# Delta-rule state without its zero blocks: 64-row products, accumulators banked by head, one state update

## Chip, core and metric

The kernel runs on one core of a Trainium2 chip. The metric is the device time of one execution in microseconds (us): 1829.12 us, the median of three runs (1828.71 to 1832.35).

## What is computed

The reference is a two-layer decoder trunk on 1024 tokens of width 1024, in float32: an RWKV-7 time-mixing layer, then a differential-attention layer, each followed by a gated per-layer input embedding (a matrix product, a sigmoid, a product), and a last RMSNorm. The change touches the recurrence of the first layer alone. There, 16 heads of 64 carry a 64 by 64 state from token to token:

```python
def step(state, inp):
    r_t, w_t, k_t, v_t, kk_t, b_t = inp
    sa = jnp.einsum('bhij,bhj->bhi', state, kk_t)
    state = (state * w_t[:, :, None, :] - sa[..., None] * b_t[:, :, None, :]
             + v_t[..., None] * k_t[:, :, None, :])
    y_t = jnp.einsum('bhij,bhj->bhi', state, r_t)
    return state, y_t
...
_, y = lax.scan(step, s0, ...)
mean = jnp.mean(y, axis=-1, keepdims=True)
var = jnp.mean(jnp.square(y - mean), axis=-1, keepdims=True)
y = ((y - mean) * lax.rsqrt(var + GN_EPS) * ln_w.reshape(H, N) + ln_b.reshape(H, N))
...
return (y * jax.nn.silu(gate)) @ w_out
```

## The kernel before

The recurrence is done in 16 chunks of 64 tokens. Inside a chunk the steps become matrix products (the delta rule's chunked form); between chunks the state is carried. The 16 heads stand as two sets (`st` 0 and 1) of four pairs (`p_`) of two heads (`h`). A pair's two states lie as two diagonal 64 by 64 blocks of one 128 by 128 block of the tile `state[st]`, and the two blocks beside them are zero.

One chunk `c` has three steps in a fixed order:

- `chain_x(c)`: the state's products (L855) write a chunk's accumulators `xy` (one 2 KB bank of PSUM for each set), and products of the chunk's masked key matrix `m` with the values `vu` are added (L864). POOL forms `spl`, the decayed state (L875), and ACT copies the result `x` out (L878).
- `chain_u(c)`: `x` is multiplied by the inverse `ti` (L890), and DVE scales the result into `vu` (L895).
- `chain_s(c)`: the new state's products `s` (L906), the state update on DVE (L910, four instructions of 64 partitions), the output's products into the other halves of `xy` (L916), and the copies of the output `y` (L923, ACT).

Other work is woven between these steps by lists with costs, and a scheduler then sets each engine's order. Two kinds matter here. `stage1(st, c + 1)` prepares the next chunk: transposes `kbt` of the keys (L175, copied by ACT into `kbn`, L176), the products `pm` (L185), which DVE masks into `m` (L188), and transposes `prt` of a key product (L162), which DVE sums into `bon` (L166). `d1_pieces` takes the outputs of two chunks, 128 tokens, after each odd chunk: a group norm on DVE (`norm`: L953 to L955, then ACT squares `y` into `ysq`, L957; `norm2`: a sum L963, twelve small instructions on 128 by 16 for the reciprocal root, L68 and L58 to L65, the scaling L966), POOL multiplies by `lnw` (L967), DVE adds (L970). Two chunks later `turn` transposes this (`ytr`, L981), DVE forms `sg` (L984), ACT and DVE split it into `gh` and `gl` (L71, L72), and 48 matmuls `op` (L75 to L77) multiply by `w_out`. Their sum is added to `x` (`xr`, L997), and ACT squares it (`h1sq`, L1001). The first chunks have 96 matmuls `pps` of another product in the place of `op`.

The tiles `pm`, `kbt`, `prt` and `ytr` share two PSUM banks (tag `t`, `bufs=2`), so each waits until the one two places ahead of it is read. Every engine runs its instructions in its program's order:

```python
pm = [ps1[0].tile([P, 4, P], F32, tag=ps1[1], name=f"pm{h}{u}", bufs=2) for h in range(2)]
...
ps = pp.tile([P, 4, P], F32, tag="t", name=f"ytr{i}{hf}", bufs=2)
```

Of the kernel before, what the change touches and what calls it, by code (L numbers as in the profile page):

```python
# [11 lines left out]
F32 = mybir.dt.float32  # L12
# [25 lines left out]
def trunk(ctx: ExitStack, tc: tile.TileContext, A, out):  # L38
# [725 lines left out]
                                       op0=ALU.mult, op1=ALU.subtract)  # L764

    def proj_N(pp, nm, ah, al, w, tag="mm", bufs=4, by_row=False, parts=2, tick=lambda n: None):
        pss = [pp.tile([P, 512], F32, tag=tag, name=f"{nm}{hf}", bufs=bufs) for hf in range(2)]
# [48 lines left out]
    with NB("d") as d, NP("psco") as pp:  # L816
# [25 lines left out]

        def chain_x(c):

            px_, ms = [], []
            vu2 = vus.pop(c)
            if c + 1 < NCH:
                vload(c + 1)
            for st in range(2):
                kkr, kbn, m = units[st, c]  # L850
                vu = vu2[:, st]
                px_.append(pp.tile([P, 4, 2, L], F32, tag="xy", name=f"xy{st}_{c}", bufs=2))
                ctx_c[st] = (half_(st), half_(1 - st), vu, px_[st])
                with tc.high_priority():
                    ms += [T.matmul(px_[st][:, p_].rearrange("p h l -> p (h l)"), lhsT=kkr[:, p_],  # L855
                                    rhs=state[st][:, p_], start=(p_ == 0), stop=False, skip_group_check=True)
                           for p_ in range(4)]
            with tc.high_priority():
                for p_ in range(4):
                    for h in range(2):  # L860
                        for st in (1, 0):
                            xs_, ys_, vu, px = ctx_c[st]
                            m = units[st, c][2]
                            ms.append(T.matmul(px[xs_, p_, h], lhsT=m[ys_, h, p_, half_(st)], rhs=vu[ys_, p_, h],  # L864
                                               start=False, stop=True, skip_group_check=True))
            turns(ms)
            x = co.tile([P, 4, 2, L], F32, tag="x", name=f"x{c}", bufs=1)
            for st in range(2):
                xs_, ys_, vu, px = ctx_c[st]
                spl = None  # L870
                if c < NCH - 1:
                    spl = co.tile([P, 4, L], F32, tag="spl", name=f"spl{st}_{c}", bufs=2)
                    for h in range(2):
                        hs = half_(h)
                        G.tensor_tensor(out=spl[hs], in0=state[st][hs, :, hs],  # L875
                                        in1=plast[hs, 4 * st:4 * st + 4, c:c + 1].to_broadcast([64, 4, L]),
                                        op=ALU.mult)
                S.copy(x[xs_], px[xs_])  # L878
                ctx_c[st] += (spl, x)

        def chain_u(c):
            ti = tis[c // 4]
            pu = [pp.tile([P, 4, 2, L], F32, tag="us", name=f"u{st}_{c}", bufs=2) for st in range(2)]
            ms = []
            with tc.high_priority():
                for p_ in range(4):
                    for h in range(2):
                        for st in (1, 0):
                            xs_, x = ctx_c[st][0], ctx_c[st][5]
                            ms.append(T.matmul(pu[st][xs_, p_, h], lhsT=ti[xs_, (c % 4) * 8 + h * 4 + p_],  # L890
                                               rhs=x[xs_, p_, h], start=True, stop=True))
            turns(ms)
            for st in range(2):
                xs_, vu = ctx_c[st][0], ctx_c[st][2]
                V.tensor_tensor(out=vu[xs_], in0=pu[st][xs_],  # L895
                                in1=rn[xs_, c].rearrange("p h j -> p j h").unsqueeze(3).to_broadcast([64, 4, 2, L]),
                                op=ALU.mult)

        def chain_s(c):
            ms = []  # L900
            if c < NCH - 1:
                for st in range(2):
                    vu, spl, kbn = ctx_c[st][2], ctx_c[st][4], units[st, c][1]
                    pS = pp.tile([P, 4, L], F32, tag="us", name=f"s{st}_{c}", bufs=2)
                    with tc.high_priority():
                        ms += [T.matmul(pS[half_(h), p_], lhsT=kbn[:, p_, half_(h)], rhs=vu[:, p_, h],  # L906
                                        start=True, stop=True) for p_ in range(4) for h in range(2)]
                    for h in range(2):
                        hs = half_(h)
                        V.tensor_tensor(out=state[st][hs, :, hs], in0=pS[hs], in1=spl[hs], op=ALU.add)  # L910
            with tc.high_priority():
                for p_ in range(4):
                    for h in range(2):
                        for st in (1, 0):
                            xs_, ys_, vu, px = ctx_c[st][:4]
                            ms.append(T.matmul(px[ys_, p_, h], lhsT=units[st, c][2][:, h, p_, half_(1 - st)],  # L916
                                               rhs=vu[:, p_, h], start=False, stop=True, skip_group_check=True))
            turns(ms)
            po = (c % 2) * 64
            for st in range(2):  # L920
                ys_, px = ctx_c[st][1], ctx_c[st][3]
                units.pop((st, c))
                S.copy(D1[c // 2]["y"][po:po + 64, st * 512:st * 512 + 512], px[ys_].rearrange("p j h l -> p (j h l)"))  # L923

        D1, wo = {}, {}

# [708 lines left out]
```

## Time and profile before

| | |
|---|---|
| median of three runs | 1829.12 us |
| the profiled execution | 1828.3 us, span 1826.5 us |
| busy: PE (matmul) | 1684.7 us, 92% of the span |
| busy: DVE | 1350.9 us, 74% |
| busy: ACT | 760.4 us, 42% |
| busy: POOL | 634.5 us, 35% |
| mean granted TensorE clock | 0.963 of full speed |
| first and last L906 (new state's products) | 602.29 and 886.37 us |

The profile is one execution. An instruction's row gives its start, its duration, its engine and line, the tile it writes and those it reads; where its engine stood idle ahead of it, the row names what ended that. A float32 matmul of the program is two passes in the trace, so 16 matmuls show as x32. Matmuls overlap each other, so their spacing is read from the rows' spans and not from one duration.

### The profile page before, as it was taken

How to read it: one execution, taken by the hardware profiler on the slowest of the kernel's cores; microseconds unless marked ns; L12 is line 12 of the kernel's file. 1: busy time of each engine (PE TensorE's matmuls, PEld its weight loads, DVE VectorE, ACT ScalarE, POOL GpSimd, SP SyncE). 2: the span in 40 equal slices, each digit the busy share in tenths (PEclk: the TensorE clock that was granted, in tenths of full speed). 3: DMA queues.
4: the chain of work that ended last, by engine and by line, in shares of the span. 5: the costliest groups of instructions: out<-in, count | busy, mean ns of one | idle time of the engine just before them, and what ended most of it. 6: DMA issues, size and time to landing. Idle time of an engine off the chain costs nothing.

```text
span 1826.5 us, 30473 instructions
## 1 busy us (share of the span) xinstructions
PE 1684.7 (92%) x11320; PEld 1397.6 (77%) x11320; DVE 1350.9 (74%) x3083; ACT 760.4 (42%) x1594; POOL 634.5 (35%) x705
## 2 busy tenths in 40 slices
PE   6899999898897988898899999899999999999998
PEld 5677778887676877777678878788888888777786
DVE  7878954698994687666766747887877878856665
ACT  6566543346344332223333434444444444544332
POOL 4436644224324355455310333323323323311200
PEclk9999999998998989999999999999999999999999
DMA  7125444434225534444243411101101101431121
GB/s 267 41 61 166 129 106 109 125 102 119 73 67 186 186 127 127 122 129 131 97 172 128 132 51 39 54 7 56 56 7 56 53 10 56 154 99 34 58 93 69
DMA packets 164401, 175.97 MB, mean 96 GB/s; under 512 B 74845, under 2 KB 127837, under 8 KB 164254
## 3 DMA queue, kind: packets, MB, share of 16 engines
q1 hardware_dynamic: 161950, 169.84, 30.2%
q10 hardware_dynamic: 2304, 4.20, 0.6%
q8 instruction: 89, 1.46, 0.4%
q14 instruction: 58, 0.48, 0.1%
HBM read 124.19 MB, written 49.81 MB: 95 GB/s over the span
## 4 chain that ended last, share of the span: by engine, by line
PE 51%; DVE 10%; ACT 2%; issue 1%; DMA 0%; POOL 0%; ACTq 0%; DVEq 0%
PE qkv L75 6%; PE qkv L76 6%; PE qkv L77 6%; PE av L1359 3%; PE sc L1319 2%; PE sc L1320 2%; PE fg L75 2%; PE fg L76 2%; PE fg L77 2%; PE op L75 2%; PE op L77 2%; PE op L76 2%; PE do L75 1%; PE pg L76 1%; PE pg L77 1%; PE do L76 1%
## 5 line engine op out<-in xcount | busy, mean ns | idle before, releaser
L1329 ACT ACTIVATE e<-sc,mx 128x256 f32<-128x256 f32 (+7 forms) x128 | 94.0, 738 | 111.0 <-DVE mx L1326 60.0
L1273 POOL TENSOR_TENSOR rp<-rp,rq 128x128 f32<-128x128 f32 x64 | 34.8, 543 | 237.6 <-DVE rq L1268 189.7
L1359 PE MATMUL av<-vh,aT 128*128 128x128 f32 x576 | 81.1, 280 | 6.3 <-DVE aT L1355 6.3
L1359 PEld LDWEIGHTS av<-vh,aT 128*128 128x128 f32 x576 | 75.6, 195 | 12.8 <-DVE aT L1355 8.9
L1325 DVE TENSOR_REDUCE mxs<-sc 128x1 f32<-128x128 f32 (+6 forms) x112 | 74.2, 682 | 0.5
L1319 PE MATMUL sc<-k,q 128*128 128x512 f32 (+2 forms) x192 | 71.5, 379 | 2.2 <-ACT e L1329 2.2
L229 DVE SCALAR_TENSOR_TENSOR xmt<-hT,cB,xmt 128x512 f32<-128x512 f32 x64 | 63.5, 1012 | 6.6 <-ACT xmt L228 6.3
L1320 PE MATMUL sc<-k,q 128*128 128x512 f32 (+2 forms) x192 | 64.8, 348 | 0.0
L1361 ACT ACTIVATE o<-av,r 128x128 f32<-128x128 f32 x64 | 23.5, 367 | 88.4 <-PE av L1359 88.4
L875 POOL TENSOR_TENSOR spl<-state,plast 64x256 f32<-64x256 f32 x60 | 41.4, 690 | 49.6 <-DVE state L910 42.7
L1341 DVE SCALAR_TENSOR_TENSOR e<-e,r,e 128x128 f32<-128x128 f32 (+3 forms) x64 | 56.5, 883 | 1.2
L560 DVE TENSOR_TENSOR tb<-tb,tm 128x31 f32<-128x31 f32 (+15 forms) x124 | 53.9, 435 | 3.6
L558 DVE TENSOR_TENSOR tm<-tb,nb 128x31 f32<-128x31 f32 (+15 forms) x124 | 53.9, 434 | 3.6
L188 DVE TENSOR_TENSOR m<-pm,mmask 128x512 f32<-128x512 f32 x64 | 41.1, 682 | 20.0 <-PE pm L185 19.7
L1301 POOL CAST q<-q 64x128 fp32r<-64x128 f32 x128 | 38.5, 302 | 49.4 <-PE sc L1320 45.6
L1267 DVE TENSOR_TENSOR rp<-qkv,rc 128x256 f32<-128x256 f32 x64 | 27.1, 423 | 38.3 <-PE qkv L77 30.1
L1292 POOL CAST k<-k 64x256 fp32r<-64x256 f32 x64 | 26.1, 408 | 83.7 <-ACT k L1290 82.5
L185 PE MATMUL pm<-kkr,kb 64*128 64x128 f32 x512 | 50.8, 307 | 3.1 <-ACT kbn L176 2.2
L1355 DVE COPY aT<-at 128x512 f32<-128x512 f32 (+2 forms) x96 | 52.0, 550 | 1.1 <-PE at L1353 0.4
L185 PEld LDWEIGHTS pm<-kkr,kb 64*128 64x128 f32 x512 | 40.4, 203 | 12.9 <-issue 6.0
L1353 PE MATMUL at<-ident,e 128*128 128x128 f32 x288 | 47.4, 277 | 2.8 <-DVE e L1341 2.3
L923 ACT COPY y<-xy 64x512 f32<-64x512 f32 x32 | 18.6, 580 | 71.4 <-PE xy L916 71.0
(1180 smaller groups left out, 6001.5 us busy)
## 6 DMA issues: line engine op xcount, KB each, us to landing
pp_d<-ppo SPq DMA_DIRECT2D x32, 256.0 KB, 2.3
kb_d<-kb SPq DMA_DIRECT2D x16, 512.0 KB, 2.6
kkr<-kkr_d SPq DMA_DIRECT2D x32, 256.0 KB, 3.2
kb<-kb_d SPq DMA_DIRECT2D x32, 256.0 KB, 3.3
x<-in_x SPq DMA_DIRECT2D x8, 512.0 KB, 5.5
kkr_d<-ep SPq DMA_DIRECT2D x16, 256.0 KB, 2.6
kkr_d<-rt SPq DMA_DIRECT2D x16, 256.0 KB, 2.6
bb<-kb_d SPq DMA_DIRECT2D x32, 128.0 KB, 2.6
```

Source lines behind the costliest of these rows:

```text
L75: T.matmul(ps, lhsT=ah, rhs=bh, start=start, stop=False)
L76: T.matmul(ps, lhsT=ah, rhs=bl, start=False, stop=False)
L77: T.matmul(ps, lhsT=al, rhs=bh, start=False, stop=stop)
L185: ms.append(T.matmul(pm[h][:, p_], lhsT=kb[hs, p_], rhs=kkr[hs, p_], start=True, stop=True))
L229: V.scalar_tensor_tensor(out=t, in0=hT[:, kt, half(hf)], scalar=cB[:, g, kt:kt + 1], in1=t, op0=ALU.mult, op1=ALU.add)
L558: V.tensor_tensor(out=tv, in0=tb[:, j:j + 1, 0:w].to_broadcast([P, n, w]), in1=nb[:, j + 1:32, j:j + 1].to_broadcast([P, n, w]), op=ALU.mult)
L1319: T.matmul(ps[:, b0:b1], lhsT=q1[:, m, ts_], rhs=k1[:, m, b0:b1], start=True, stop=False)
L1320: T.matmul(ps[:, b0:b1], lhsT=q0[i % 2][:, m], rhs=k2[:, b0:b1], start=False, stop=True)
L1325: V.tensor_reduce(out=seed, in_=ps[:, 0:n - P], axis=AX.X, op=ALU.min)
L1329: S.activation(e[:, 0:n], ps[:, 0:n], AF.Exp, scale=-1.0, bias=mx, accum_out=l_[:, m:m + 1])
L1341: V.scalar_tensor_tensor(out=es[0][:, 0:n], in0=es[1][:, 0:n], scalar=r[:, 1:2], in1=es[0][:, 0:n], op0=ALU.mult, op1=ALU.add)
L1359: T.matmul(po, lhsT=aT[kb // 4][:, kb % 4], rhs=c["vh"][:, kb], start=(kb == 0), stop=(kb == i))
```

## The change

The tile `state` holds only the diagonal blocks: 128 partitions (the two heads of a pair in the lower and the upper 64) by two sets, four pairs and 64 columns. The state's products become 16 matmuls on 64 rows and 64 columns in place of 8 on 128 and 128, the two heads in turns. The accumulators `xy` are one tile of two banks, split by head and no longer by set, with `bufs=1`. The state update, and `spl` on POOL, become one instruction on 128 partitions each. The copies of `x` and `y` read across the two banks. `proj_N` takes a two-bank tile where its tag is `xy`.

```diff
-        state = []
-        for st in range(2):
-            s_ = co.tile([P, 4, P], F32, name=f"state{st}")
-            G.memset(s_, 0.0)
-            state.append(s_)
+        state = co.tile([P, 2, 4, L], F32, name="state")
+        G.memset(state, 0.0)
...
-                px_.append(pp.tile([P, 4, 2, L], F32, tag="xy", name=f"xy{st}_{c}", bufs=2))
...
-                    ms += [T.matmul(px_[st][:, p_].rearrange("p h l -> p (h l)"), lhsT=kkr[:, p_],
-                                    rhs=state[st][:, p_], start=(p_ == 0), stop=False, skip_group_check=True)
-                           for p_ in range(4)]
+            px = pp.tile([P, 2, 2, 4, L], F32, tag="xy", name=f"xy{c}", bufs=1)
             with tc.high_priority():
...
+                for st in range(2):
+                    kkr = units[st, c][0]
+                    for p_ in range(4):
+                        for h in range(2):
+                            ms.append(T.matmul(px[:, h, st, p_], lhsT=kkr[half_(h), p_], rhs=state[half_(h), st, p_],
+                                               start=(st == 0 and p_ == 0), stop=False, skip_group_check=True))
+                for h in range(2):
+                    for p_ in range(4):
+                        for st, h_ in ((1, h), (0, 1 - h)):
+                            ms.append(T.matmul(px[half_(st), h_, st, p_],
+                                               lhsT=units[st, c][2][half_(1 - st), h_, p_, half_(st)],
+                                               rhs=vu2[half_(1 - st), st, p_, h_],
                                                start=False, stop=True, skip_group_check=True))
             turns(ms)
...
+                spl = co.tile([P, KT, L], F32, tag="spl", name=f"spl{c}", bufs=2)
+                G.tensor_tensor(out=spl, in0=state.rearrange("p s j l -> p (s j) l"),
+                                in1=plast[:, :, c:c + 1].to_broadcast([P, KT, L]), op=ALU.mult)
...
-                    for h in range(2):
-                        hs = half_(h)
-                        V.tensor_tensor(out=state[st][hs, :, hs], in0=pS[hs], in1=spl[hs], op=ALU.add)
+                pS = pp.tile([P, 2, 4, L], F32, tag="us", name=f"s{c}", bufs=2)
...
+                V.tensor_tensor(out=state, in0=pS, in1=spl.rearrange("p (s j) l -> p s j l", s=2), op=ALU.add)
```

The scheduler also orders the work around these steps anew. Three places in the recurrence show it; numbers in a tile's name tell its chunk and its buffer, and the changed kernel's line numbers differ by a few (L855 is now L856, L864 is L861, L890 is L886, L906 is L901, L916 is L908, L923 is L916, L966 is L959).

The first is DVE's queue in chunk 6, an even chunk, behind the sum `gst<-ysq` of the group norm. `gst` are the norm's small statistics, `m_6` the mask products that chunk 6's L864 reads. Before:

```order
L963 TENSOR_REDUCE gst_7046<-ysq_7050 128x16
L188 TENSOR_TENSOR m_6_6625<-pm_6_6755,mmask 128x512
L188 TENSOR_TENSOR m_6_6625<-pm_6_6754,mmask 128x512
L68 TENSOR_SCALAR gst_7046<-gst_7046 128x16
L984 SCALAR_TENSOR_TENSOR sg_6601<-ytr_6825,vecs,sg_6601 128x128 x4
L58 TENSOR_SCALAR gst_7046<-gst_7046 128x16
L60 TENSOR_SCALAR gst_7046<-gst_7046 128x16
```

Now, after the sum and nine of the twelve small instructions:

```order
L63 TENSOR_TENSOR gst_7037<-gst_7037 128x16
L64 SCALAR_TENSOR_TENSOR gst_7037<-gst_7037 128x16
L65 SCALAR_TENSOR_TENSOR gst_7037<-gst_7037 128x16
L959 TENSOR_TENSOR y_6408<-y_6408,gst_7037 128x1024
L188 TENSOR_TENSOR m_6_6618<-pm_6_6751,mmask 128x512
L188 TENSOR_TENSOR m_6_6618<-pm_6_6750,mmask 128x512
L963 TENSOR_TENSOR y_6408<-y_6408,vn_7031 128x1024
L977 SCALAR_TENSOR_TENSOR sg_6594<-ytr_6817,vecs,sg_6594 128x128 x4
```

The two `m` have moved from directly behind the sum to behind all twelve small instructions and the scaling of `y` (L966, now L959), and `sg` to behind the addition L970 (now L963). Chunks 2, 4, 12 and 14 now read the same; in chunks 8 and 10 seven small instructions stand ahead of the first `m`, one between the two, and the scaling behind them. Before, `m` stood directly behind the sum in chunks 6, 8, 12 and 14, ahead of the sum in 4 and 10, and behind one and two small instructions in 2.

The second is PE's queue at the entry of chunk 7, an odd chunk. Before, behind the last product of chunk 6 (here a matmul of L916):

```order
L916 MATMUL xy_6_6867<-vu_6627,m_6_6621 64x64
L162 MATMUL prt_7_6940<-ident,pr_7_6937 128x128 x2
L175 MATMUL kbt_7_6975<-ident,kbp_7_6973 128x128 x4
L76 MATMUL op_6912<-rwo7l,gh_6783 128x512
L77 MATMUL op_6912<-rwo7h,gl_6784 128x512
L77 MATMUL op_7116<-rwo0h,gl_6784 128x512
```

Then 16 more `op`, the state's products, and the eight `pm`, of which the last two open this piece:

```order
L185 MATMUL pm_7_7029<-kkr_7_6860,kb_7_6861 128x128
L185 MATMUL pm_7_7028<-kkr_7_6860,kb_7_6861 128x128
L76 MATMUL op_7116<-rwo6l,gh_6783 128x512
L77 MATMUL op_7116<-rwo6h,gl_6784 128x512
L75 MATMUL op_7116<-rwo7h,gh_6783 128x512
L76 MATMUL op_7116<-rwo7l,gh_6783 128x512
L77 MATMUL op_7116<-rwo7h,gl_6784 128x512
L162 MATMUL prt_7_7055<-ident,pr_7_7052 128x128 x2
L864 MATMUL xy_7_7076<-vu_6864,m_7_6862 64x64
```

Now:

```order
L76 MATMUL op_7110<-rwo7l,gh_6779 128x512
L77 MATMUL op_7110<-rwo7h,gl_6780 128x512
L856 MATMUL xy_7062<-state,kkr_7_6848 128x64 x8
L856 MATMUL xy_7062<-state,kkr_7_6852 128x64 x8
L162 MATMUL prt_7_6935<-ident,pr_7_6932 128x128 x2
L175 MATMUL kbt_7_6970<-ident,kbp_7_6968 128x128 x4
L185 MATMUL pm_7_7020<-kkr_7_6852,kb_7_6853 128x128
L185 MATMUL pm_7_7019<-kkr_7_6852,kb_7_6853 128x128
```

All 48 `op` now stand ahead of the state's products (19 of them already ahead of chunk 6's L890, 21 behind it, 8 behind L916). `prt` and `kbt` have moved behind the state's products, directly ahead of `pm`, and behind the eight `pm` come only `prt` and the L864 products (now L861).

The third is ACT's queue from the output copies of chunk 4 to the first `kbn` of chunk 6. Before:

```order
L923 COPY y_6414<-xy_4_6431 64x512
L923 COPY y_6414<-xy_4_6426 64x512
L176 COPY kbn_5_6422<-kbt_5_6534 128x512
L1001 ACTIVATE h1sq_6752,ss_5440<-xr_6127 128x1024
L878 COPY x_6656<-xy_5_6635 64x512
L878 COPY x_6656<-xy_5_6630 64x512
L176 COPY kbn_6_6622<-kbt_6_6669 128x512
```

Now:

```order
L916 COPY y_6408<-xy_6420 64x2x4x64 x2
L994 ACTIVATE h1sq_6748,ss_5440<-xr_6122 128x1024
L176 COPY kbn_5_6416<-kbt_5_6531 128x512
L873 COPY x_6658<-xy_6623 64x512 x2
L176 COPY kbn_6_6615<-kbt_6_6665 128x512
```

`h1sq`, which reads the sum of all 48 `op`, has moved from behind `kbn_5` to ahead of it. Each later odd chunk reads the same.

## Rows read from the trace of the kernel before

**Rows 1.** Busy time by engine over the recurrence; columns: stretch, length, PE, PEld, DVE, ACT, POOL, clock, DMA:

```profile
588.00:911.00 323.00, 284.00 (x3378) 239.34 (x3376) 226.76 (x443) 93.99 (x148) 159.37 (x164) 0.94 0.42 131
```

**Rows 2.** What PE waited for there: us in total, times, longest:

```profile
PE ytr L981 <- DVE m L188: 16.8, 6, 4.1
...
PE xy L855 <- ACT y L923: 5.2, 1, 5.2
```

**Rows 3.** Timeline, chunk 5's products to chunk 6's; columns: start, duration, engine:

```profile
696.78 1.15 PE L864 MATMUL xy<-vu,m 64*64 64x64 f32 x32
...
701.79 1.15 PE L906 MATMUL s<-vu,kbn 128*64 128x64 f32 x32 [0.32 <-DVE vu L895]
...
702.86 1.77 DVE L910 TENSOR_TENSOR state<-s,spl 64x256 f32<-64x256 f32 x4
...
703.91 1.18 ACT L923 COPY y<-xy 64x512 f32<-64x512 f32 x2 [4.23 <-PE xy L916]
...
704.54 2.05 PE L855 MATMUL xy<-state,kkr 128*128 128x128 f32 x16
...
705.55 1.22 DVE L953 TENSOR_REDUCE gst<-y 128x16 f32<-128x1024 f32 x1
...
709.72 1.22 DVE L963 TENSOR_REDUCE gst<-ysq 128x16 f32<-128x1024 f32 x1 [1.18 <-ACT ysq L957]
710.97 1.29 DVE L188 TENSOR_TENSOR m<-pm,mmask 128x512 f32<-128x512 f32 x2
711.72 0.82 PE L981 MATMUL ytr<-ident,y 128*128 128x128 f32 x4 [4.04 <-DVE m L188]
...
712.47 1.98 PE L864 MATMUL xy<-vu,m 64*64 64x64 f32 x32
712.58 1.12 DVE L984 SCALAR_TENSOR_TENSOR sg<-ytr,vecs,sg 128x128 f32<-128x128 f32 x4 [0.24 <-PE ytr L981]
713.63 0.16 DVE L58 TENSOR_SCALAR gst<-gst 128x16 int32<-128x16 int32 x1
713.74 0.63 ACT L71 ACTIVATE gh<-sg 128x512 fp32r<-128x512 f32 x1 [4.05 <-DVE sg L984]
713.82 0.17 DVE L60 TENSOR_SCALAR gst<-gst 128x16 int32<-128x16 int32 x1
...
714.86 0.91 PE L981 MATMUL ytr<-ident,y 128*128 128x128 f32 x4
```

**Rows 4.** Timeline, the rest of chunk 6 and the entry of chunk 7:

```profile
721.20 1.23 DVE L966 TENSOR_TENSOR y<-y,gst 128x1024 f32<-128x1024 f32 x1
...
722.57 2.40 POOL L967 TENSOR_TENSOR y<-y,lnw 128x1024 f32<-128x1024 f32 x1 [3.89 <-DVE y L966]
...
725.26 1.15 PE L906 MATMUL s<-vu,kbn 128*64 128x64 f32 x32
...
727.91 0.48 PE L76 MATMUL op<-rwo7l,gh 128*128 128x512 f32 x1
...
732.09 0.40 PE L75 MATMUL op<-rwo6h,gh 128*128 128x512 f32 x1
...
734.21 1.16 PE L185 MATMUL pm<-kkr,kb 64*128 64x128 f32 x16
...
735.40 1.29 DVE L188 TENSOR_TENSOR m<-pm,mmask 128x512 f32<-128x512 f32 x2 [5.90 <-PE pm L185]
...
736.86 1.15 PE L864 MATMUL xy<-vu,m 64*64 64x64 f32 x32
...
737.52 1.06 ACT L1001 ACTIVATE h1sq<-xr 128x1024 f32<-128x1024 f32 x1 [8.34 <-issue]
```

**Rows 5.** Timeline, the new state's products of chunks 3 and 13:

```profile
663.72 1.39 PE L906 MATMUL s<-vu,kbn 128*64 128x64 f32 x32
...
866.02 1.15 PE L906 MATMUL s<-vu,kbn 128*64 128x64 f32 x32 [0.31 <-DVE vu L895]
```

**Rows 6.** Timeline, small products in another stage of the kernel:

```profile
562.59 2.06 PE L593 MATMUL po<-prhs,pairs 64*64 64x32 f32 x64
```

More of the change, by code (lines that the diff above doesn't have):

```diff
@@ L766, in proj_N @@
     def proj_N(pp, nm, ah, al, w, tag="mm", bufs=4, by_row=False, parts=2, tick=lambda n: None):
-        pss = [pp.tile([P, 512], F32, tag=tag, name=f"{nm}{hf}", bufs=bufs) for hf in range(2)]
+        if tag == "xy":
+            t = pp.tile([P, 2, 512], F32, tag=tag, name=nm, bufs=1)
+            pss = [t[:, hf] for hf in range(2)]
+        else:
+            pss = [pp.tile([P, 512], F32, tag=tag, name=f"{nm}{hf}", bufs=bufs) for hf in range(2)]
         if parts == 3:
@@ L843, in chain_x @@
         def chain_x(c):
-            px_, ms = [], []
+            ms = []
             vu2 = vus.pop(c)
@@ L865, in chain_x @@
                                                start=False, stop=True, skip_group_check=True))
             turns(ms)
-            x = co.tile([P, 4, 2, L], F32, tag="x", name=f"x{c}", bufs=1)
-            for st in range(2):
[L869 to L873, printed above, removed]
-                        hs = half_(h)
[L875 to L879, printed above, removed]
+            spl = None
@@ new lines, in chain_x @@
+            if c < NCH - 1:
+                spl = co.tile([P, KT, L], F32, tag="spl", name=f"spl{c}", bufs=2)
+                G.tensor_tensor(out=spl, in0=state.rearrange("p s j l -> p (s j) l"),
+                                in1=plast[:, :, c:c + 1].to_broadcast([P, KT, L]), op=ALU.mult)
+            x = co.tile([P, 2, 4, L], F32, tag="x", name=f"x{c}", bufs=1)
+            for st in range(2):
+                S.copy(x[half_(st)], px[half_(st), :, st])
+            ctx_c[0] = (vu2, px, spl, x)
@@ L881, in chain_u @@
         def chain_u(c):
+            vu2, px, spl, x = ctx_c[0]
             ti = tis[c // 4]
@@ L888, in chain_u @@
                         for st in (1, 0):
-                            xs_, x = ctx_c[st][0], ctx_c[st][5]
+                            xs_ = half_(st)
                             ms.append(T.matmul(pu[st][xs_, p_, h], lhsT=ti[xs_, (c % 4) * 8 + h * 4 + p_],
-                                               rhs=x[xs_, p_, h], start=True, stop=True))
+                                               rhs=x[xs_, h, p_], start=True, stop=True))
             turns(ms)
             for st in range(2):
-                xs_, vu = ctx_c[st][0], ctx_c[st][2]
-                V.tensor_tensor(out=vu[xs_], in0=pu[st][xs_],
+                xs_ = half_(st)
+                V.tensor_tensor(out=vu2[xs_, st], in0=pu[st][xs_],
                                 in1=rn[xs_, c].rearrange("p h j -> p j h").unsqueeze(3).to_broadcast([64, 4, 2, L]),
@@ L899, in chain_s @@
         def chain_s(c):
+            vu2, px, spl, x = ctx_c[0]
             ms = []
             if c < NCH - 1:
[L902 to L909, printed above, removed]
-                        V.tensor_tensor(out=state[st][hs, :, hs], in0=pS[hs], in1=spl[hs], op=ALU.add)
+                pS = pp.tile([P, 2, 4, L], F32, tag="us", name=f"s{c}", bufs=2)
+                with tc.high_priority():
+                    ms += [T.matmul(pS[half_(h), st, p_], lhsT=units[st, c][1][:, p_, half_(h)], rhs=vu2[:, st, p_, h],
+                                    start=True, stop=True) for st in range(2) for p_ in range(4) for h in range(2)]
+                V.tensor_tensor(out=state, in0=pS, in1=spl.rearrange("p (s j) l -> p s j l", s=2), op=ALU.add)
             with tc.high_priority():
@@ L914, in chain_s @@
                         for st in (1, 0):
-                            xs_, ys_, vu, px = ctx_c[st][:4]
-                            ms.append(T.matmul(px[ys_, p_, h], lhsT=units[st, c][2][:, h, p_, half_(1 - st)],
-                                               rhs=vu[:, p_, h], start=False, stop=True, skip_group_check=True))
+                            ms.append(T.matmul(px[half_(1 - st), h, st, p_],
+                                               lhsT=units[st, c][2][:, h, p_, half_(1 - st)],
+                                               rhs=vu2[:, st, p_, h], start=False, stop=True, skip_group_check=True))
             turns(ms)
             po = (c % 2) * 64
+            yv = D1[c // 2]["y"].rearrange("p (s j h l) -> p s h j l", s=2, h=2, l=L)
             for st in range(2):
-                ys_, px = ctx_c[st][1], ctx_c[st][3]
                 units.pop((st, c))
-                S.copy(D1[c // 2]["y"][po:po + 64, st * 512:st * 512 + 512], px[ys_].rearrange("p j h l -> p (j h l)"))
+                S.copy(yv[po:po + 64, st], px[half_(1 - st), :, st])
         D1, wo = {}, {}
```

10 lines of the change are left out of this document (removed).

## The prediction

> **What bounds the kernel now.** First the busy time by stretch: the change touches the recurrence alone, 323 us of the span, in which PE is busy for 284 us (88%), DVE for 227 and POOL for 159 [rows 1]. No engine is full, so orders and waits decide, beside PE's work. Next the waits of PE: the largest is `ytr` for the mask products `m`, 16.8 us in six waits [rows 2], one for each even chunk from 4 on. Last the timeline of one pair of chunks, 5 to 7. Read it as one chain. The new state's products start at 701.79. The output copies end at 705.09 and the group norm starts at 705.55; its sum L963 ends at 710.94, `m` takes 710.97 to 712.26, and PE, 4.04 us idle, goes on with `ytr` and at 712.47 with L864 [rows 3]. So in an even chunk **DVE's queue from the norm to `m`** releases PE. From L864 of chunk 6 to L864 of chunk 7 (736.86) 24.39 us go by [rows 3, 4], nearly all of it matmuls. From L864 to a chunk's new state's products it is 5.0 us in chunk 5, with no `h1sq` ahead of the `x` copies (696.78 to 701.79 [rows 3]); in chunk 7 `h1sq` runs from 737.52 to 738.58 [rows 4] and comes ahead of them.
>
> Five pairs, from 663.72 to 866.02, take 202.30 us [rows 5]; one holds a wait of 5.2 us for an ACT copy [rows 2], whose cause (weights that ACT must scale first) stays. Without it a pair takes (202.30 - 5.2) / 5 = 39.4 us.
>
> **The parts, priced.** *State's products.* Before, 16 passes of 128 by 128 took 2.05 us, the last one's latency included [rows 3], about 1.9 of throughput. Now 32 passes of 64 rows and 64 columns. Their price is not in the trace. From below: 64 passes of 64 by 64 weights on 32 columns, in turns, took 2.06 us, about 0.03 each [rows 6]. From above: 16 passes of 64 rows on 128 columns, in turns, took 1.16 us, about 0.06 each [rows 4]. The L906 products, 32 passes on 64 columns in 1.15 us [rows 4], are nearest in columns, so I take 0.03: 1.0 us, a saving of 0.9 a chunk; the other end saves nothing.
>
> *State update.* Four instructions of 1.77 us together [rows 3] become one on 128 by 512, priced as one `m` (1.29 / 2 = 0.65). It must wait for all 32 passes of L906, so it ends about 703.7 in place of 704.63. What follows on DVE needs the output copies (705.09), so the norm starts at 705.2, **0.35 earlier**, not 1.0. The single `xy` buffer makes the next state's products wait for both copies, 705.1 in place of 704.54; in an even chunk they end far ahead of `m`, and in an odd one `op` covers it: nothing. `spl` on POOL shortens; POOL has room: nothing. The `xy` tile of `proj_N` serves every other projection, with a whole projection between two uses: nothing; if that cover failed, a few tenths of a us at each of four.
>
> *DVE's new order, chunks 4, 6, 12, 14.* The sum ends at 710.6. Twelve small instructions at 0.2 (713.63 to 713.82 [rows 3]) make 2.4, the scaling L966 1.23 [rows 4]: 714.25. Then `m`, 1.29: 715.55, and L864 at 715.75, **3.3 us later** than now. `sg` waits for more: POOL's product (2.40, some 0.14 behind the scaling [rows 4]) and DVE's addition (128 by 1024, as L966): 718.05; `sg` takes 1.12, `gh` 0.63 [rows 3]. So PE does L864 and `prt` until 718.15 (712.47 to 714.86, where `ytr` now starts [rows 3]), waits for `sg` until 719.2 because the second `ytr` needs its bank, and starts `op` at 719.9.
>
> From there PE has: 19 `op` at 0.23 (19 rows from 727.91 to 732.09 [rows 4]), 4.4; L890 1.0; `kbt` and one `pm` 0.6; 21 `op` 4.8; L906 and L916 2.0; six `pm` 0.45; 8 `op` 1.85; the state's products 1.0; `prt` and `kbt` 0.6 (the last two with L906 and L916 are 725.26 to 727.91 now [rows 4]). That is 736.8. Now the entry of chunk 7 turns against it. `kbn` stands behind `h1sq`, and that behind the sum of the last `op`: the addition 0.7, `h1sq` 1.06 and its read-out 0.19, `kbn` 0.6 end at 737.9. The second `pm` bank waits for `kbn`; then `pm` and `m` as now, 734.21 to 736.69 [rows 4], 2.5 us, with no `op` left to cover `m`: L864 of chunk 7 at 740.5 in place of 736.86. Then 5.0 us, `h1sq` being out of the way. The pair's period is 740.5 - 701.79 + 5.0 = **43.7 us**.
>
> *Chunks 8 and 10.* Seven small instructions (1.4), `m`, one small one, `m`: 713.5, L864 at 713.7. `sg` needs no addition now and is ready at 715.25; PE starts `op` at 716.75 (2.4 for L864 and `prt`, 0.65 for `ytr`), 3.15 earlier than above. Period 40.55.
>
> *The ends.* Chunks 0 and 1, where nothing holds PE between the state's products and the next: -0.9 each. Pair 1 to 3: `m` moved the same way, but 12 `pps` cover most of it: I take +0.7 (between -0.9, all covered, and +3.3, nothing). Chunk 15: twelve small statistics of the next stage and two sums `bon`, some 3.3 us from the end of `h1sq`, now stand ahead of `m`, which could start 1.8 behind it: +1.5.
>
> **Sum.** Six pairs: 4 x 43.7 + 2 x 40.55 = 255.9, against 6 x 39.4 = 236.4: +19.5. Ends +0.4. In all +19.9 on the profiled execution's 1828.3 (span 1826.5 and 1.8 around it): 1848.2; this execution lies 0.8 below the median, so 1849 on the median's scale. A measurement tells about 0.2% (3.7 us) from no change.
>
> **Rivals.** *R1, faster: PE's own work decides.* If PE were never held by `m` longer than now, each chunk would lose 0.9: 16 x 0.9 = 15, 1814. For it: PE is 88% busy. Against: PE can pass `m` only if `m` is masked by 712.26, and the queue has 3.6 us more ahead of it. Chance 0.15.
>
> *R2, no change: the order's delay costs once and the waits behind it dissolve.* PE's matmuls from L864 to L864 then take about 21.3 (24.39 less 0.9 and some 2 of waits); periods 715.75 - 701.79 + 21.3 + 5.0 = 40.3 and 38.2; six pairs +1, ends +0.4: 1830, between 1824 and 1836. For it: L864 to L864 is nearly full now. Against: `sg` behind the addition, and `kbn` behind `h1sq`, are waits that no row hides. Chance 0.15, a third of it faster, half the same.
>
> *R3, slower still: the change's halves don't run side by side.* Then 32 passes cost 0.06 each, 1.9 us, and nothing is saved: +0.9 in chunks 0 to 2 and some 0.7 in each odd chunk: about 1856. For it: each product still loads 128 columns of weights, and there are twice as many. Against: `pm` loads as many for each pass and takes 0.06 with twice the moving columns [rows 4]. Chance 0.12. The Trainium skill, TensorE: Matmul & The Clock Gate, section "LDWEIGHTS (loading the stationary operand)", speaks for this rival: a load's time goes by columns and not by rows, about 107 ns for 128. By that rule two sets of 16 loads would need an estimated 1.7 us, a saving of 0.2 and not 0.9. The trace does not bear it out: 16 `pm` passes, each with such a load, took 1.16 us in all [rows 4], 0.07 each.
>
> **How the numbers follow.** My forecast has 0.58, mostly 1840 to 1860: the waits behind `sg` and `kbn` (1 to 2 us each, six times) could be half as long, or the clock could stay low longer after PE's idle time, now up to 8 us. R1 0.15, R2 0.15, R3 0.12. Range 1822 to 1864: it takes in R2 and R3 and leaves out R1 and a tail above. The forecast's own range is 1839 to 1858. Faster by over 0.2%: 0.15 + 0.05 = 0.20; the same: 0.08; slower: 0.58 + 0.12 + 0.02 = 0.72.
>
> **What would show it.** Right: `ytr` waits for `m` some 7 to 8 us in chunks 4, 6, 12 and 14 and 5 to 6 in 8 and 10, about 40 in all in place of 16.8; 12 small instructions and the scaling between the norm's sum and `m`; L185 waiting for `kbn` in odd chunks; the state's 32 passes in about 1.2 us; one state update of about 0.7. Wrong: the waits for `m` no longer than now (R1), L864 to L864 in 21 to 22 us (R2), or 32 passes in 2 us (R3).

## The result and the profile after

The changed kernel took **1890.38 us** (median of 4 runs, 1888.73 to 1893.49) against 1830.47 (4 runs, 1828.71 to 1832.35): ratio 1.033, 95% interval 1.0316 to 1.0343. The forecast was 1849: the direction was right, the size was not, 60 us in place of 20, and the time lies outside the range of 1822 to 1864. The profiled execution took 1890.8 (span 1889.0).

First the whole recurrence, and then the stretch around one long wait in its chunk 6; columns: busy time of PE, PEld, DVE, ACT and POOL, then the granted clock, DMA share, GB/s:

```profile
592.00:973.00 381.00, 306.68 (x3670) 255.47 (x3669) 220.20 (x411) 96.54 (x149) 128.05 (x121) 0.87 0.38 119
728.00:745.00 17.00, 12.28 (x98) 9.78 (x99) 10.88 (x28) 2.32 (x5) 3.69 (x3) 0.63 0.21 62
```

The same stage took 323 us at a granted clock of 0.94 [rows 1]; now 381 at 0.87. DVE and POOL work less than before. PE's busy time rose by 23 us with as many columns to move as before (256 passes more, of half the width); the other 35 us are idle time. What PE waited for there (us in total, times, longest):

```profile
PE ytr L974 <- DVE m L188: 37.8, 6, 7.7
PE xy L856 <- ACT y L916: 11.6, 7, 6.7
PE prt L162 <- DVE m L188: 8.9, 9, 1.9
PE pm L185 <- issue: 5.3, 2, 2.7
PE u L886 <- ACT x L873: 5.0, 7, 3.1
```

The first row was 16.8, the second 5.2 [rows 2]. The pair of chunks that the prediction walked, 5 to 7, on PE:

```profile
718.55 1.15 PE L901 MATMUL s<-vu,kbn 128*64 128x64 f32 x32 [0.41 <-DVE vu L891]
...
721.91 2.00 PE L856 MATMUL xy<-state,kkr 64*128 64x64 f32 x32 [0.47 <-ACT y L916]
732.28 1.11 PE L974 MATMUL ytr<-ident,y 128*128 128x128 f32 x4 [7.42 <-DVE m L188]
733.32 1.97 PE L861 MATMUL xy<-vu,m 64*64 64x64 f32 x32
736.35 1.11 PE L974 MATMUL ytr<-ident,y 128*128 128x128 f32 x4 [0.44 <-DVE sg L977]
743.22 1.15 PE L886 MATMUL u<-x,ti 64*64 64x64 f32 x32
750.71 1.15 PE L901 MATMUL s<-vu,kbn 128*64 128x64 f32 x32
755.63 2.00 PE L856 MATMUL xy<-state,kkr 64*128 64x64 f32 x32
761.00 0.41 PE L162 MATMUL prt<-ident,pr 128*128 128x128 f32 x2 [0.73 <-DVE m L188]
761.51 1.15 PE L861 MATMUL xy<-vu,m 64*64 64x64 f32 x32
766.62 1.15 PE L901 MATMUL s<-vu,kbn 128*64 128x64 f32 x32 [0.41 <-DVE vu L891]
```

Three things are to be seen. The 32 passes of 64 rows take 2.00 us, as long as the 16 passes of 128 rows did (2.05 [rows 3]). PE stands 7.42 us for `m`. And the pair lasts 766.62 - 718.55 = 48.07 us. DVE in front of `m`:

```profile
726.51 1.22 DVE L956 TENSOR_REDUCE gst<-ysq 128x16 f32<-128x1024 f32 x1 [1.18 <-ACT ysq L950]
727.76 0.17 DVE L68 TENSOR_SCALAR gst<-gst 128x16 f32<-128x16 f32 x1
...
730.06 0.18 DVE L65 SCALAR_TENSOR_TENSOR gst<-gst 128x16 f32<-128x16 f32 x1
730.27 1.23 DVE L959 TENSOR_TENSOR y<-y,gst 128x1024 f32<-128x1024 f32 x1
731.53 1.29 DVE L188 TENSOR_TENSOR m<-pm,mmask 128x512 f32<-128x512 f32 x2
734.03 1.23 DVE L963 TENSOR_TENSOR y<-y,vn 128x1024 f32<-128x1024 f32 x1 [1.21 <-POOL y L960]
735.17 1.12 DVE L977 SCALAR_TENSOR_TENSOR sg<-ytr,vecs,sg 128x128 f32<-128x128 f32 x4
```

Twelve small instructions and the scaling, 3.8 us with their starts, stand between the sum and `m`, as the order said. And PE behind that wait (its `op`, some rows of it):

```profile
737.69 0.63 PE L76 MATMUL op<-rwo0l,gh 128*128 128x512 f32 x1
738.12 0.63 PE L75 MATMUL op<-rwo0h,gh 128*128 128x512 f32 x1
...
740.63 0.39 PE L75 MATMUL op<-rwo2h,gh 128*128 128x512 f32 x1
740.86 0.39 PE L76 MATMUL op<-rwo2l,gh 128*128 128x512 f32 x1
```

After 7.42 us of idleness a pass comes every 0.43 us until 740.6, then every 0.23: the granted clock of the stretch is 0.63 of full speed, a part of it at 1.2 GHz and the rest at 2.4.

Where the span's 62.5 us lie, by starts of the new state's products: from chunk 3 to 13 five pairs went from 202.30 [rows 5] to 906.58 - 671.23 = 235.35, **+33.1**; from chunk 13's to chunk 15's output products, 908.05 - 866.02 = 42.0 before, it is 966.41 - 906.58 = 59.8, **+17.8**; up to chunk 3 +7.5; behind chunk 15 +4.1. Two of these need care. Of the 7.5, 4.6 came before the recurrence began (562.59 [rows 6] against 567.15); but that row starts anywhere from 562.59 to 565.11 in the profiles of the seven kernels with the old products and from 562.88 to 567.15 in the others, so no effect of the change can be told there. And the marks at the end do not part the same work: behind chunk 15's output products PE still had 92 `op` before and has 76 now. Some 3.7 us of the +17.8 (16 at 0.23) is thus work that used to come later, and the rest of the program lost more than its +4.1 says. Chunk 15 shows a wait of its own, on ACT and on PE:

```profile
956.81 1.15 ACT L721 ACTIVATE pwg<-pwg04r,vecs 128x1024 fp32r<-128x1024 f32 x1 [9.85 <-DMA pwg05r<-in_pwg]
957.87 1.16 ACT L873 COPY x<-xy 64x512 f32<-64x512 f32 x2
```

```profile
959.08 1.97 PE L886 MATMUL u<-x,ti 64*64 64x64 f32 x32 [3.07 <-ACT x L873]
```

A row of the next stage's gate weights, waiting for its DMA, stands ahead of the copies of `x`; in the kernel before it stood behind them.

### The profile page after: what moved, and what is told of

Read it like the earlier page. It is cut to its first block, busy times and chain, and to the rows that moved or that the text cites. A ratio compares the mean times of both kernels' runs of the same rounds, so it can differ in the third digit from the quotient of the medians.

```text
span 1889.0 us, 30854 instructions
## 1 busy us (share of the span) xinstructions
PE 1701.2 (90%) x11576; PEld 1408.1 (75%) x11576; DVE 1334.9 (71%) x3038; ACT 759.9 (40%) x1594; POOL 595.5 (32%) x659
## 4 chain that ended last, share of the span: by engine, by line
PE 51%; DVE 11%; issue 2%; ACT 2%; DMA 1%; POOL 0%; SPq 0%; ACTq 0%; DVEq 0%; POOLq 0%
PE qkv L75 6%; PE qkv L76 6%; PE qkv L77 6%; PE av L1352 3%; PE op L75 2%; PE sc L1312 2%; PE sc L1313 2%; PE fg L75 2%; PE fg L77 2%; PE fg L76 2%; PE op L76 2%; PE op L77 1%; PE pm L185 1%; PE do L75 1%; PE do L77 1%
## 5 line engine op out<-in xcount | busy, mean ns | idle before, releaser
L185 PE MATMUL pm<-kkr,kb 64*128 64x128 f32 x512 | 54.1, 317 | 9.8 <-issue 5.3
L185 PEld LDWEIGHTS pm<-kkr,kb 64*128 64x128 f32 x512 | 43.3, 213 | 19.2 <-issue 11.2
L188 DVE TENSOR_TENSOR m<-pm,mmask 128x512 f32<-128x512 f32 x64 | 41.3, 682 | 22.3 <-PE pm L185 19.9
L974 PE MATMUL ytr<-ident,y 128*128 128x128 f32 x64 | 14.7, 379 | 43.2 <-DVE m L188 37.8
L171 POOL TENSOR_TENSOR kbp<-kb,plast 128x512 f32<-128x512 f32 x32 | 33.6, 1049 | 52.1 <-PE kbt L175 51.5
```

The lines of the kernel that those rows point to most:

```text
L185: ms.append(T.matmul(pm[h][:, p_], lhsT=kb[hs, p_], rhs=kkr[hs, p_], start=True, stop=True))
```

## Experiments

`turns([a, b])` puts b behind a on the engine (no wait is added); a name such as marks["m", 1, c, h] is the recorded instruction. An edit fixes only the order that it names; the scheduler orders the rest around it anew. All ratios are to the kernel before on the same chip, with 95% intervals. Runs 1 to 4, 5 to 8 and 9 to 14 stand on three chips, on which the kernel before took 1829.8, 1830.2 and 1828.7 us, so times of different groups compare to within some 1.5 us.

**1 and 2: VectorE's order, undone in the changed kernel and put into the kernel before.** Run 1 holds the norm's small operations behind `vu` in the even chunks 2 to 14, further back than they stood in the kernel before; run 2 touches chunks 2, 4, 6, 12 and 14.

```diff
 # 1, changed kernel, norm2():
+                e_ = mean_eps(st[:, 1], st[:, 1], L, 64e-5)
+                if i < 7:
+                    for b in range(2):
+                        turns([marks["vu", 2 * i + 2, b], e_])
 # 2, kernel before, norm2(), behind the scaling e_:
+                if i in (0, 1, 2, 5, 6):
+                    for b in marks["m", 1, 2 * i + 2]:
+                        turns([e_, b])
```

> The changed kernel with VectorE's order of the kernel before in the even chunks: the twelve small operations and the scaling of the group norm are held behind the two evictions of u of that chunk, so the mask products come right behind the sum. Theory A (the lost time is VectorE's order, and the low clock that follows its long waits): ytr's waits for m fall from 37.8 us to 15 to 20 us, the granted clock of the stage rises from 0.87 to 0.92 or more, and the time falls by 35 to 50 us, to 1840 to 1855. Theory B (the products on 64 rows and the one accumulator are what costs, by waits of theirs): the time falls by less than 15 us and stays above 1875. If the order were all of it and the change saved what the forecast put down for the products, it would be 1820 or less.

> The kernel before with VectorE's order of the changed kernel in chunks 2, 4, 6, 12 and 14: the small operations and the scaling of the norm are put ahead of the two mask products; nothing else is changed. Theory A: ytr waits for m 30 us or more in all, the time rises by 20 to 45 us, to 1850 to 1875, without any of the new products. Theory B: it rises by less than 10 us.

Measured: run 1 1868.57 us (1.0211, 1.0196 to 1.0226), 21.8 under the changed kernel; run 2 1864.73 us (1.0191, 1.0176 to 1.0206), 35.0 over the kernel before. The waits for `m`, of run 1 and of run 2:

```profile
PE ytr L979 <- DVE m L190: 20.0, 6, 3.9
```

```profile
PE xy L867 <- DVE m L190: 33.0, 6, 7.8
```

Run 2 is inside theory A's numbers: the order of the norm, with the old products, loses 35 us. It is not VectorE's order alone, though, for TensorE's changed with it: all `op` now stand ahead of the state's products, and `prt` and `kbt` directly ahead of `pm`, as in the changed kernel. An odd chunk of run 2:

```profile
750.59 1.27 PE L187 MATMUL pm<-kkr,kb 64*128 64x128 f32 x16 [0.56 <-PE kbt L177]
752.60 0.41 PE L164 MATMUL prt<-ident,pr 128*128 128x128 f32 x2 [0.73 <-DVE m L190]
```

Run 14 below puts this part at some 0.5 us a pair, in the changed kernel. Run 1 falls between the theories: the wait came back to about what it was, but the clock rose only from 0.87 to 0.89, and 38 us are left. The order is a large part and not the whole.

**3 and 4: the mask products first, in both kernels.** The norm's first reduction waits in the order for both `m`; in run 3 the edit of run 1 stays.

```diff
+                e_ = V.tensor_reduce(out=st[:, 0], in_=y3, axis=AX.X, op=ALU.add)
+                if i < 7:
+                    for h in range(2):
+                        turns([marks["m", 1, 2 * i + 2, h], e_])
```

> As the first run of this set, and the sum, the subtraction and the square's sum of the group norm also held behind the mask products of the chunk, so that the mask products come first on VectorE. Theory A: ytr's waits for m all but vanish (under 6 us in the stage), and the time is 10 to 20 us under the first run's: 1820 to 1840. Theory B: above 1865.

> The kernel before with the whole group norm held behind the mask products of the chunk. Theory A (what VectorE does ahead of the mask products is what TensorE waits for): the 16.8 us of waits for m fall under 6 us and the time falls by 8 to 20 us, to 1810 to 1822. Rival: the waits only move to the next thing that VectorE does later (gl, the evictions of u), and the time stays within 4 us of 1830.

Measured: run 3 1856.48 us (1.0145, 1.0128 to 1.0162); run 4 1822.65 us (0.9961, 0.9946 to 0.9976), and again in run 12. In both, `ytr` now waits 4.7 us for `m` in all. So an order alone takes the wait away in either kernel, and it is worth 7 us in the kernel before and 12 in the changed one. But with the mask products first in both, the changed kernel is still 34 us behind: theory A's 1820 to 1840 was missed.

**5 and 6: the gate weights behind chunk 15's copies of `x` and `gh`.**

```diff
+    def late(b):
+        for k in (("x", 0), ("x", 1), ("gh", 0), ("gh", 1)):
+            if k in marks:
+                turns([marks[k], b])
 ...
-            S.activation(h, r, AF.Copy, scale=scale)
+            late(S.activation(h, r, AF.Copy, scale=scale))
```

> The changed kernel with the mask products first (as in the third run) and, on ScalarE, the next layer's gate weights (pwg) held behind chunk 15's copies of x and the two gh of that chunk; in the third run the copies of x stood 9.6 us behind a gate row that waited for its DMA. Theory A' (what is left of the loss at the end of the stage is this place in ScalarE's queue): u's wait for x in chunk 15 falls from 3.3 us to under 1 and the time by 4 to 10 us, to 1846 to 1852. Rival (the end of the stage is set by the norm of the last chunks and by what TensorE still has to do): within 3 us of 1856.

> The kernel before with the mask products first (as in the fourth run) and the gate weights held behind the same copies and gh; there the copies of x stood ahead of the gate row already, and only gh waited behind it (3.9 us). Theory A': 1818 to 1822, at most 4 us under the fourth run. Rival: within 1 us of 1822.7, since the op that waited has other work behind it.

Measured: run 5 1854.99 us (1.0131, 1.0116 to 1.0146), run 6 1828.51 (0.9989, 0.9979 to 0.9999). The wait of `u` in chunk 15 is gone in run 5, the time is not: the rival holds. Run 6 met neither: it is 6 us above run 4. That late gate weights are paid for behind the stage, where they are needed, fits the profiles and is not shown: behind chunk 15's output products run 5 took 931.7 us and run 3 927.8, run 6 917.4 and run 4 912.2.

**7 and 8: 32 and 128 moving columns in a pass over the state.** Run 7 leaves out half of each product, run 8 adds the next head's state to it; each was timed once.

```diff
-  px[:, h, st, p_], ..., rhs=state[half_(h), st, p_]
+  px[:, h, st, p_, 0:32], ..., rhs=state[half_(h), st, p_, 0:32]
+  px[:, h, st, min(p_, 2):min(p_, 2) + 2], ..., rhs=state[half_(h), st, min(p_, 2):min(p_, 2) + 2]
```

> The changed kernel in which each of the 32 passes over the state moves 32 columns in place of 64 (columns 32 to 63 of every head are left out of that product). If the load of 128 weight columns sets the pace of a pass, the 32 passes still take 1.9 to 2.05 us; if the moving columns set it, about 1.0 us.

> The changed kernel in which each of the 32 passes moves 128 columns in place of 64 (the next head's state is added to the product as well, which is then not the reference's). If the weight load sets the pace and the two row halves do run side by side, the 32 passes still take 2.0 to 2.2 us; if the moving columns set it, or the two halves run one after the other, about 4 us.

A typical row of run 7, and of run 8:

```profile
720.78 1.97 PE L856 MATMUL xy<-state,kkr 64*128 64x32 f32 x32 [0.47 <-ACT y L916]
```

```profile
717.08 2.06 PE L856 MATMUL xy<-state,kkr 64*128 64x128 f32 x32 [0.47 <-ACT y L916]
```

32, 64 and 128 moving columns take 1.97, 2.00 and 2.06 us. Up to 128 the moving columns do not set the pace of these passes; what the three have in common is 128 weight columns of 64 rows in each pass. The whole times, 1889.99 and 1892.3, are those of the changed kernel.

**9: the last transposes of `y` behind the first gate product**, in run 5's kernel.

```diff
+                    if i == NT - 1 and hf == q == 0:
+                        turns([marks["pg0"], a_])
```

> The fifth run's kernel (mask products first, gate weights late), and on TensorE the transposes of the last y (row tile 7) held behind all 48 passes of the first gate product; in the fifth run they stood in the middle of it and waited 4.7 us for the norm. Theory A'' (the end and what follows it cost by the places in the queues): the wait is covered, the time falls by 3 to 6 us, to 1849 to 1852. Rival (what waits is the norm itself, and op behind it runs later by as much): within 2 us of 1855.

Measured: 1853.04 us (1.0132, 1.0119 to 1.0145): the rival, at its edge. The 4.7 us wait for `y` went, and one of 4.3 us for the last gate weight came.

**10: the state update joined over the two sets, alone**, in run 4's kernel: state, `spl` and the accumulator `s` in one tile each for both sets (`spl` with one buffer in place of two), the update in two instructions in place of four. The zero blocks, the products and `xy` stay.

```diff
-                    for h in range(2):
 ...
-                        V.tensor_tensor(out=state[st][hs, :, hs], in0=pS[hs], in1=spl[hs], op=ALU.add)
+                for h in range(2):
 ...
+                    V.tensor_tensor(out=state2[hs, :, :, hs], in0=pS[hs], in1=spl[hs], op=ALU.add)
```

> The fourth run's kernel (before, mask products first) with the state of both sets in one tile and one accumulator, and its update in two operations for all heads in place of four; zero blocks, products and xy accumulators as before. If the joint update is harmless: within 3 us of the fourth run, 1819 to 1826. If the joint update (or its single accumulator for both sets' new states) is a part of the loss: 1830 or more.

Measured: 1825.10 us (0.9978, 0.9966 to 0.9991), within 3 us of run 4. Joining the update is harmless and worth nothing that can be told. The change's one instruction needs the state without its zero blocks and was not run by itself.

**11: the zero blocks put back into the changed kernel** (run 3's order): 32 passes of full height with 64 moving columns, the state updated in two instructions.

```diff
-  lhsT=kkr[half_(h), p_], rhs=state[half_(h), st, p_],
+  lhsT=kkr[:, p_], rhs=state[:, st, p_, half_(h)],
```

> The third run's kernel (changed, mask products first) with the zero blocks put back: 32 passes of 128 rows, 128 weight columns and 64 moving columns, accumulators banked by head as in the change; the state is updated in two operations. If 128 weight columns set the pace whatever the rows, the 32 passes take 1.9 to 2.0 us and the time is within 4 us of the third run's 1856.5: leaving out the zero rows then bought nothing, and the loss that is left belongs to the banked accumulators. If 64 rows side by side did save, the passes take 2.5 us or more here and the time is 10 us or more above 1856.

Measured: 1871.44 us (1.0236, 1.0218 to 1.0253), 15 over run 3. A row of it:

```profile
769.72 3.79 PE L859 MATMUL xy<-state,kkr 128*128 128x64 f32 x32 [0.47 <-ACT y L924]
```

The first theory fell. A pass of 128 rows and 128 weight columns takes 3.79 / 32 = 0.118 us, one of 64 rows 2.00 / 32 = 0.0625: the two row halves do run side by side. That a pass costs simply by its rows, one behind the other, is a rival that no run tests; against it stand the weight loads, which take as long at half height (a median of 188 ns for 64 rows in the changed kernel, 192 for 128 in the kernel before). With runs 7 and 8: a pass costs some 0.12 us of its half of the array for its 128 weight columns, and two halves go at once. The kernel before had 16 such passes of full height, 16 x 0.12 = 1.9; the change has 32 of half height, two at a time, 32 x 0.06 = 1.9.

**12: run 4 again.**

> The fourth run's kernel once more, with more rounds: faster than the kernel before by 0.2 to 0.5 per cent (1821 to 1826), if its first result was not one chip's; the rival is no difference, within 0.1 per cent.

Measured: 1822.68 us (0.9971, 0.9959 to 0.9983; 12 runs). The kernel before with the mask products first is faster than both kernels of this document.

**13 and 14: what is left in the pairs, the cover of `op`.** Run 13 holds the products with the state behind the last `op` in run 12's kernel; run 14 holds the last nine passes of `op` behind `kbt` in run 9's.

```diff
 # 13, mms():
+                if hf == 1 and k0 + 2 == KT and i < 5:
+                    turns([a_, marks["xs", 2 * i + 5]])
 # 14, mms():
+                    if hf == 1 and kt == 5 and i < 5:
+                        turns([marks["kbt", 1, 2 * i + 5], firsts[0]])
```

> The twelfth run's kernel (before, mask products first) with TensorE's order of the changed kernel in the odd chunks 5 to 13: the whole of op stands ahead of the products with the state, and none is left between kbt and the key products that wait for ScalarE and VectorE. Theory O (what is left between the two kernels in the pairs, 2.4 us per pair, is the lost cover): the pair period rises from 37.3 to about 39.5 us and the time by 6 to 12 us, to 1829 to 1835. Rival (the banked accumulators and the 32 passes cost it themselves): within 3 us of 1822.7.

> The ninth run's kernel (changed, mask products first, gate weights and the last transposes late) with the last nine passes of op held behind kbt in the odd chunks 5 to 13, where the kernel before has them. Theory O: the pair period falls from 39.5 towards 37.5 us, and the time by 5 to 12 us, to 1841 to 1848; what is left over the kernel before then lies in the first chunk and behind the stage. Rival: within 3 us of 1853.

Measured: run 13 1821.12 us (0.9957, 0.9941 to 0.9973), no loss. But its edit did not give the order that it was made for: the scheduler moved `prt` and `kbt` ahead too, so that two to seven `op` and the state's products still stand between `kbt` and `pm`, and `pm` does not wait:

```profile
769.43 0.63 PE L177 MATMUL kbt<-ident,kbp 128*128 128x128 f32 x4 [0.19 <-DVE m L190]
...
771.52 1.95 PE L858 MATMUL xy<-state,kkr 128*128 128x128 f32 x16
773.40 1.16 PE L187 MATMUL pm<-kkr,kb 64*128 64x128 f32 x16
```

So run 13 leaves theory O untested in the kernel before. Run 14 1847.99 us (1.0104, 1.0091 to 1.0118), 5 us better than run 9, the low end of what O said; but its pair went only from 39.40 to 38.95 us, where O wanted 37.5. A pair of run 14, chunks 7 to 9 on PE, some of its waits:

```profile
744.69 1.15 PE L914 MATMUL s<-vu,kbn 128*64 128x64 f32 x32 [0.41 <-DVE vu L904]
748.04 2.00 PE L867 MATMUL xy<-state,kkr 64*128 64x64 f32 x32 [0.46 <-ACT y L929]
751.77 0.66 PE L993 MATMUL ytr<-ident,y 128*128 128x128 f32 x4 [0.78 <-DVE m L198]
754.53 0.65 PE L993 MATMUL ytr<-ident,y 128*128 128x128 f32 x4 [0.64 <-DVE sg L998]
757.12 0.50 PE L80 MATMUL op<-rwo0h,gl 128*128 128x512 f32 x1 [0.73 <-DVE gl L72]
...
783.64 1.15 PE L914 MATMUL s<-vu,kbn 128*64 128x64 f32 x32 [0.41 <-DVE vu L904]
```

and of run 13, the same pair:

```profile
743.62 1.15 PE L910 MATMUL s<-vu,kbn 128*64 128x64 f32 x32 [0.32 <-DVE vu L899]
750.29 0.65 PE L988 MATMUL ytr<-ident,y 128*128 128x128 f32 x4 [0.78 <-DVE m L190]
752.75 0.33 PE L894 MATMUL u<-x,ti 64*64 64x64 f32 x2 [0.35 <-ACT x L882]
...
780.89 1.15 PE L910 MATMUL s<-vu,kbn 128*64 128x64 f32 x32 [0.32 <-DVE vu L899]
```

38.95 against 37.27 us. The difference, 1.7, can be read: the idle times in PE's rows of the pair add up to 4.2 us in run 14 and to 2.5 in run 13. Run 14 waits 0.46 for the copies of `y`, both of which the single accumulator needs, and 0.64 + 0.73 for `sg` and `gl`; in run 13 the `u` products come first, with a wait of 0.35 for `x`, and `sg` and `gl` are ready behind them.

## Why the prediction was wrong

**Right.** What bounds the even chunks, and what the new order does to it: six waits for `m` of 37.8 us in all (about 40 forecast), 7.4 to 7.7 in chunks 4, 6 and 14 (7 to 8), 5.1 and 4.8 in 8 and 10 (5 to 6), though 5.4 in 12 (7 to 8); the twelve small instructions and the scaling ahead of `m`, L861 14.8 us behind the new state's products (14.0). The single state update took 0.69 us (0.65), and the joined one of run 10 changed nothing that can be told. Run 2 shows that the norm's order makes the kernel slower without any of the new products.

**Where the error lies.** The span rose by 62.5 us in place of 19.9. The gap of 42.6 is 17.9 in the five pairs (33.1 against 3 x 4.3 + 2 x 1.15 = 15.2), 12.0 from chunk 13 to 15 (17.8 against 4.3 + 1.5), 8.6 up to chunk 3 (7.5 against -1.1, with the 4.6 before the recurrence in it) and 4.1 behind, where the sum had nothing.

**The step that failed first: the price of the state's products**, "so I take 0.03: 1.0 us, a saving of 0.9 a chunk". The passes took 0.0625 each, 2.00 us, and nothing was saved. In the prediction's own sum this price is worth some 7 us, R3's 1856, and not 0.9 in each chunk: in the even chunks the products end far ahead of `m`. The bounds were right and the choice between them was wrong: I took the row with as many moving columns (L906, 64), but runs 7 and 8 show that these passes do not feel the moving columns, and the nearest row was the `pm` of [rows 4], with 128 weight columns and 64 rows, 0.07. Rival R3 had this price with 0.12 of the chances, but its mechanism was wrong: the halves do run side by side (run 11). I had set the `pm` row against this price, where two halves run side by side as well. The Trainium skill, TensorE: Matmul & The Clock Gate, section "LDWEIGHTS (loading the stationary operand)", has a load's time go by its columns and not by its rows, by its formula an estimated 107 ns for 128. This case agrees that the rows do not count (188 and 192 ns for loads of 64 and 128 rows, run 11), but not in the figure: passes of full height, each with such a load, came every 118 ns, and the loads themselves last longer and overlap. The estimate of 1.7 us that the prediction drew from that rule lies nearer to the 2.00 measured than the 1.0 that it took.

**The second: PE's work behind the wait at its full pace.** The pair 5 to 7 was forecast at 43.7 and took 48.07. Half of the 4.4 is there at `u`, which stood 24.7 us behind the new state's products and not 22.5: the first 19 `op` behind the wait were counted at 0.23, 4.4 us, but came at 0.43 until 740.6 and took 6.1. The other half is the walk from there on, counted too tight: from `u` to the new state's products 7.5 us in place of 6.4, to the state's products 4.9 in place of 4.3, to L861 5.9 in place of 5.5; the dearer products can be no more than the last 0.4. I had put "the clock could stay low longer" into the range and not into the sum, though the wait that brings it was in the sum. The other pairs were not walked, and their part of the 17.9 is not shown to have this cause. L185 waiting for `kbn` in the odd chunks was not what the rows show: in chunk 7 its wait is 0.56 and names `kbt`, ending 0.10 us behind the sum `bon` (758.90) and ahead of the end of `kbn` (759.07), and `m` behind it is uncovered for 0.73.

**The third: "chunk 15: +1.5"**, with 4.3 for chunk 14 before it: 5.8 against 17.8, or against 14 without the 16 `op` that moved ahead. The whole end moved: the low clock in chunk 15 as well (L861 1.98 us, L886 1.97), a wait of 2.54 at `pm`, and ACT standing 9.85 us for the gate weights' DMA ahead of `x`. The wait at `pm`, on PE, and the sum on DVE that reads the bank it needs:

```profile
948.88 2.08 PE L185 MATMUL pm<-kkr,kb 64*128 64x128 f32 x16 [2.54 <-issue]
```

```profile
947.92 0.86 DVE L166 TENSOR_REDUCE bon<-prt 64x4 f32<-64x256 f32 x2
```

The row names no releaser, but `bon` ended at 948.78, 0.10 ahead of `pm`, as in chunk 7, and it stands behind eight of the next stage's twelve small statistics: the prediction had these ahead of `m`, and they hold up `pm` already. Taking away the last wait, that of `u` for `x`, gained nothing that can be told (run 5, on run 3's order), so it is a place and not shown to be a cause.

**The account.** Of the 60 us, holding back the norm's small operations took away 22 (run 1); the same order put into the kernel before cost it 35, with the order of TensorE that came with it (run 2). Holding back the rest of the norm ahead of `m` took away 12 more (run 3), but the kernel before gains 7 from that too (run 4). The `op` held behind `kbt` took away 5 (run 14). With all that mended the changed kernel is still 27 us behind run 13 (1847.99 against 1821.12; 23.7 in the profiled spans, 1844.1 and 1820.4). About 9 of these lie in the five pairs (666.89 to 869.43 against 668.05 to 861.42, 202.5 and 193.4 us): 1.0 to 1.9 in each of the first four, waits like those shown with run 14, and 3.3 in the last. The accumulators banked by head, with the old products, were not run by themselves. Some 14 lie behind chunk 15's output products (916.64 to 1844.1 against 907.47 to 1820.4, 927.5 and 912.9 us; three `op` more stand there, 0.7 us):

```profile
917.00:937.00 20.00, 13.89 (x74) 10.68 (x71) 13.31 (x24) 9.46 (x12) 3.63 (x2) 0.74 0.83 288
937.00:957.00 20.00, 15.80 (x69) 12.21 (x68) 9.36 (x15) 3.71 (x6) 4.67 (x2) 0.91 0.16 52
```

```profile
908.00:928.00 20.00, 17.39 (x96) 13.56 (x93) 15.14 (x26) 10.84 (x13) 6.39 (x3) 1.00 0.73 241
928.00:948.00 20.00, 18.49 (x88) 14.74 (x87) 9.66 (x21) 4.58 (x8) 1.07 (x1) 1.00 0.20 76
```

These are the first 40 us behind the last chunk, run 14 above and run 13 below: less busy, and a clock of 0.74 and 0.91 in place of 1.00. PE waits there for the next stage's first rows (4.5 us, 1.4 in run 13) and its last gate weight (3.4). What makes them later was tried in runs 5 and 9 without success, and **stays open**.

## What to carry to other kernels

Price a matmul pass from a row with the same weight columns and the same height of the array, not with the same moving columns: here leaving out zero rows halved the height and doubled the passes, and where the weights set the pace that gains nothing. Where a planner orders the engines, a smaller cost in one place is a new order everywhere: look for what now stands ahead of the instruction that the busiest engine waits for, and pin it; here that alone made the unchanged kernel 6 us faster (run 12), where the change had made it 60 slower. Look at the other engines' orders again behind such a pin. And a wait of many microseconds on PE is not its length: add the work behind it at the lower clock.

## What the runs showed that was not expected

- 32, 64 and 128 moving columns cost the same in a pass of 64 rows and 128 weight columns: 1.97, 2.00 and 2.06 us for 32 passes.
- Two passes on different row halves run side by side, as the rows read: 0.0625 us each against 0.118 for full height.
- An order put in on one engine changed another's: run 2's on VectorE took the cover from `pm` on TensorE, and run 13's left it there, against its purpose.
- A wait of 3.3 us taken off the end of the stage (run 5) and one of 4.7 (run 9) gained 1.5 and 2.0 us, no more than these measurements tell: another wait stood behind each.
